# Sixteen of 22 gate-and-up column pairs of a SwiGLU feed-forward as seven block products instead of eight, in a float32 encoder trunk on one core

## The chip, the cores and the metric

The kernel runs on one core of one Trainium2 chip. Its time is the time on the device, in microseconds, from one launch; the median of three runs before the change is 2384.12 us (2383.22 to 2384.5). A profile of one execution goes with it.

## The reference

The program is an encoder trunk over one sequence of 512 tokens with 1024 features, all in float32. Two layers run one after the other. Each has a feed-forward, a mixer (a two-way state-space scan in the first layer, neighbourhood attention in the second), a second feed-forward, and a gated input from a side embedding:

```python
def rmsnorm(x, g):
    y = xf * lax.rsqrt(jnp.mean(xf * xf, axis=-1, keepdims=True) + RMS_EPS)
    return (y * g.astype(jnp.float32)).astype(x.dtype)

def swiglu(x, w_gu, w_down):
    g, u = jnp.split(x @ w_gu, 2, axis=-1)
    return (jax.nn.silu(g) * u) @ w_down

for i in range(DEPTH):                                        # DEPTH = 2
    h = h + 0.5 * swiglu(rmsnorm(h, ffn1_norm[i]), ffn1_w_gu[i], ffn1_w_down[i])
    hn = rmsnorm(h, mix_norm[i])
    h = h + (ssd_mixer(hn, ...) if i % 2 == 0 else neighbourhood_attention(hn, ...))
    h = h + 0.5 * swiglu(rmsnorm(h, ffn2_norm[i]), ffn2_w_gu[i], ffn2_w_down[i])
    gate = jax.nn.sigmoid(rmsnorm(h, ple_norm[i]) @ ple_w_gate[i])
    h = h + gate * rmsnorm(p[i] @ ple_w_proj[i], ple_post_norm[i])
```

The change concerns `swiglu`, which runs four times. `w_gu` is 1024 x 5632 (2816 gate columns, then 2816 up columns), `w_down` is 2816 x 1024.

## The kernel before

**Layout.** Features lie on the 128 partitions, tokens along the free axis. The residual stream is eight tiles `h[0..7]` of 128 x 512 (names `hs` in the profile). A weight "unit" is a 128 x 1024 tile: eight 128 x 128 blocks side by side.

**Three matmuls for one.** To keep float32 accuracy on a faster number format, each operand is held as a sum of two rounded parts, high and low. `split_unit` has ScalarE (ACT) cast a raw unit `wr` to its high part `wh` (line 166) and VectorE (DVE) subtract that from the raw unit to give the low part `wl` (line 168). Activations are split the same way into the two halves of an `md` tile (lines 189 and 190; with a gain, lines 192 and 193). For each 128 x 128 block `gemm` then issues three matmuls into one PSUM bank `ps`: high x high (line 181), weight high x activation low (line 184), weight low x activation high (line 185). TensorE (PE) takes its instructions strictly in order, so a low part that is late stops it at every third matmul.

**Weights.** `plan` lists all units in the order of use. `load_unit` issues the load of a unit on SyncE's DMA queue (SP) into one of four `wr` buffers. `unit()` hands out the next split unit and keeps up to three of them split ahead; `wh` and `wl` have three buffers each, so the split of a unit waits until the unit three before it is used up.

**A feed-forward.** The 2816 hidden columns are 22 tiles of 128, in chunks of 8, 7 and 7. For a tile f, `gate_up(f)` runs one gate unit and one up unit over the eight pairs of `norm.pairs` (the residual times the norm's gain, split), 24 matmuls of 128 x 512 each, into two banks. `activate` multiplies both by the factor `R` (one over the root mean square, in a tile `rt`; DVE, lines 313 and 317), applies SiLU on ACT (line 315), multiplies the two on GpSimd (POOL, line 318), and splits the result into `mids[f]`. `down(c)` multiplies the finished tiles of chunk c with `w_down`, one output tile d at a time, and adds half of it to `h[d]` (line 328). Chunk c's `down` runs after the gate and up units of chunk c+1. In the last `down`, `nxt(d)` prepares the next stage at once: it splits `h[d]` times the next gain and adds its square to a sum (ACT line 213, POOL line 217).

**The norm's factor.** `norm.factor()` sums over partitions with one plain float32 matmul (line 221) and runs a Newton iteration on 128 x 512 values. `norm.begin()` and `norm.end()` do the same on 128 x 4 values, with four small matmuls before (line 231) and four after it (line 241). Before, three of the feed-forwards use `factor`; the very first uses `begin` and `end`.

**Order.** The Tile framework puts the instructions of each engine into an order by their place in the code and by its own estimate of when they can run, assigns buffers from pools (24 `md`, 15 `sc`, 7 `t`, five PSUM banks of one tag and three of another), and makes the semaphores.

Of the kernel before, what the change touches and what calls it, by code (L numbers as in the profile page):

```python
# [21 lines left out]
CHUNKS = ((0, 8), (8, 15), (15, 22))  # L22
# [21 lines left out]
VAR = (0, 1, 1, 2)  # L44


@with_exitstack
def trunk(ctx, tc, A, out):
# [72 lines left out]
    def plan():  # L121
        for i in range(stop):
            l, w = divmod(i, 4)
            if w in (0, 2):
                gu, dn = (A["w_gu1"][l], A["w_dn1"][l]) if w == 0 else (A["w_gu2"][l], A["w_dn2"][l])
                for c, (a, b) in enumerate(CHUNKS):
                    for f in range(a, b):
                        yield gu[f, 0]
                        yield gu[f, 1]
                    for a, b in CHUNKS[max(c - 1, 0):c] + CHUNKS[-1:] * (c == len(CHUNKS) - 1):  # L130
                        if w == 2 and b == NF:
                            for n in range(2):
                                yield A["w_proj"][l, n]
                        for d in range(KD):
                            yield dn[d, :, a * P:b * P]
            elif w == 3:
                for n in range(KD):
                    yield A["w_gate"][l, n]
            elif l % 2 == 0:
                for n in range(65):  # L140
                    yield A["w_in"][n]
                for x in range(2):
                    for d in range(KD):
                        yield A["w_out"][d, :, x * 1024:(x + 1) * 1024]
            else:
                for n in range(24):
                    yield A["w_qkv"][n]
                for d in range(KD):
                    yield A["w_ao"][d]

    todo, raws, ready, splits = plan(), [], [], []

    def load_unit():
        src = next(todo, None)
# [6 lines left out]
    def split_unit():  # L161
        load_unit()
        if raws:
            raw, n = raws.pop(0)
            hi = wp.tile([P, 1024], F32R, name=nm("wh"), tag="wh", bufs=3)
            splits.append(s.copy(out=hi[:, :n], in_=raw[:, :n]))  # L166
            lo = wp.tile([P, 1024], F32R, name=nm("wl"), tag="wl", bufs=3)
            v.tensor_sub(out=lo[:, :n], in0=raw[:, :n], in1=hi[:, :n])  # L168
            ready.append((hi, lo))

    def unit():
        while len(ready) < 3 and (raws or not ready):
            split_unit()
        return ready.pop(0)

# [1002 lines left out]
```

## Time and profile before

| | |
|---|---|
| median of three runs | 2384.12 us |
| profiled execution, own time | 2384.19 us |
| its span, first to last instruction | 2382.4 us |
| matmuls on PE | 11464, PE busy 99% of the span |
| DVE, ACT, POOL busy | 59%, 40%, 19% |
| mean granted TensorE clock | 0.999 |
| DMA | 265.58 MB, mean 111 GB/s |

The profiled execution stands 0.07 us above the median of the runs; 1.8 us of its time lie outside the span. Matmuls are pipelined, so a matmul's own duration (392 ns for 128 x 512) is longer than the distance from one to the next, and PE's busy share says little; the distance between starts in the timeline is the better measure. "x3152" in a row is a count; the brackets in a timeline row give the idle time before it and what ended it.

### The profile page before, as it was taken

Reading aid. Unit: us, or ns where it says so; the run is one execution under the profiler, and the core shown is the slowest. Engines: PE = TensorE matmul, PEld = TensorE weight load, DVE = VectorE, ACT = ScalarE, POOL = GpSimd, SP = SyncE. Lnnn points to the kernel's source line nnn. Section 1 sums busy time; section 2 is a strip of 40 time slices with the busy share of each in tenths; the row PEclk is TensorE's granted clock in tenths of the full one; section 3 lists DMA queues with packets and bytes.
Section 4 is the critical chain, followed back from the end, with each engine's and each line's share of the span. In section 5 each row is a group of like instructions: output and inputs, shape, how many; then the busy total and the mean of one; then the engine's idle time right before and its main releaser. Section 6 shows DMA issues by size and latency. Waiting matters only on the chain.

```text
span 2382.4 us, 29262 instructions
## 1 busy us (share of the span) xinstructions
PE 2368.6 (99%) x11464; PEld 1953.0 (82%) x11464; DVE 1414.6 (59%) x1893; ACT 957.3 (40%) x1560; POOL 443.3 (19%) x373
## 2 busy tenths in 40 slices
PE   9999999999999999999999999999999999999999
PEld 8888888888888888888888788888877888888887
DVE  6453447877777858554446755444568855544456
ACT  5222324655555653322224433222337753322242
POOL 1110100444555541110103111000100011100120
PEclk9999999999999999999999999999999999999999
DMA  5333233544444452333333233333433332233332
GB/s 180 98 96 99 90 119 104 169 134 142 142 141 139 157 166 89 98 97 97 95 104 102 80 97 97 98 97 93 138 111 136 98 100 92 95 99 97 106 89 80
DMA packets 89707, 265.58 MB, mean 111 GB/s; under 512 B 10960, under 2 KB 11856, under 8 KB 89568
## 3 DMA queue, kind: packets, MB, share of 16 engines
q1 hardware_dynamic: 89280, 263.56, 35.0%
q8 instruction: 90, 1.47, 0.3%
q14 instruction: 49, 0.40, 0.1%
q10 hardware_dynamic: 288, 0.14, 0.0%
HBM read 253.40 MB, written 10.26 MB: 111 GB/s over the span
## 4 chain that ended last, share of the span: by engine, by line
PE 93%; DVE 4%; ACT 2%; issue 1%; DMA 1%; SPq 0%; POOL 0%; DVEq 0%; ACTq 0%; POOLq 0%
PE ps L181 28%; PE ps L184 28%; PE ps L185 28%; PE ps L657 1%; DVE wl L168 1%; PE ps L635 1%; PE ps L678 1%; PE ps L591 1%; PE ps L577 1%; PE ps L958 1%; PE ps L948 0%; DVE md L193 0%; DVE md L190 0%; PE ps L905 0%; PE ps L939 0%
## 5 line engine op out<-in xcount | busy, mean ns | idle before, releaser
L181 PE MATMUL ps<-md,wh 128*128 128x512 f32 (+1 forms) x3152 | 1236.7, 392 | 3.1 <-ACT md L192 3.1
L185 PE MATMUL ps<-md,wl 128*128 128x512 f32 (+1 forms) x3152 | 1228.5, 390 | 0.7 <-DVE wl L168 0.7
L184 PE MATMUL ps<-md,wh 128*128 128x512 f32 (+1 forms) x3152 | 1227.9, 390 | 0.3 <-DVE md L193 0.3
L166 ACT CAST wh<-wr 128x1024 fp32r<-128x1024 f32 (+1 forms) x401 | 414.7, 1034 | 1019.6 <-PE ps L184 638.7
L181 PEld LDWEIGHTS ps<-md,wh 128*128 128x128 f32 x3152 | 592.3, 188 | 128.2 <-issue 4.2
L184 PEld LDWEIGHTS ps<-md,wh 128*128 128x128 f32 x3152 | 592.3, 188 | 125.2 <-issue 4.9
L185 PEld LDWEIGHTS ps<-md,wl 128*128 128x128 f32 x3152 | 592.2, 188 | 124.9 <-DVE wl L168 1.3
L168 DVE TENSOR_TENSOR wl<-wr,wh 128x1024 fp32r<-128x1024 f32 (+1 forms) x401 | 576.8, 1438 | 157.5 <-ACT wh L166 131.8
L318 POOL TENSOR_TENSOR t<-t,sc 128x512 f32<-128x512 f32 x88 | 122.7, 1396 | 1033.0 <-ACT wh L166 635.4
L217 POOL TENSOR_TENSOR sq<-sq,sq 128x512 f32<-128x512 f32 x71 | 104.9, 1478 | 602.6 <-ACT sq L213 600.2
L317 DVE TENSOR_TENSOR t<-ps,rt 128x512 f32<-128x512 f32 x88 | 60.7, 690 | 258.6 <-PE ps L185 258.6
L328 DVE SCALAR_TENSOR_TENSOR hs<-ps,hs 128x512 f32<-128x512 f32 x96 | 66.3, 691 | 233.0 <-PE ps L185 233.0
L313 DVE TENSOR_TENSOR t<-ps,rt 128x512 f32<-128x512 f32 x88 | 60.8, 690 | 127.9 <-PE ps L185 125.6
L517 DVE SCALAR_TENSOR_TENSOR t<-ps,ccw,t 128x510 f32<-128x510 f32 (+1 forms) x180 | 134.0, 745 | 3.1 <-ACT t L513 0.3
L570 POOL TENSOR_TENSOR sc<-sc,sc 128x512 f32<-128x512 f32 x64 | 98.1, 1552 | 66.3 <-ACT sc L560 66.2
L189 ACT CAST md<-t 128x512 fp32r<-128x512 f32 x96 | 59.4, 623 | 121.3 <-POOL t L318 119.3
L558 ACT ACTIVATE sc<-hs,md 128x128 f32<-128x128 f32 x256 | 82.4, 396 | 2.9 <-DMA hs<-crow 2.9
L190 DVE TENSOR_TENSOR md<-t,md 128x512 fp32r<-128x512 f32 x96 | 67.9, 711 | 18.9 <-ACT md L189 18.4
L192 ACT ACTIVATE md<-hs,cst 128x512 fp32r<-128x512 f32 x64 | 46.0, 723 | 50.2 <-DVE hs L798 19.8
L520 ACT ACTIVATE t<-t 128x512 f32<-128x512 f32 x48 | 30.2, 630 | 78.6 <-DVE t L517 78.0
L585 POOL TENSOR_TENSOR md<-md,md 128x256 f32<-128x256 f32 x64 | 45.9, 751 | 84.1 <-ACT md L581 84.1
L193 DVE SCALAR_TENSOR_TENSOR md<-hs,cst,md 128x512 fp32r<-128x512 f32 x64 | 50.6, 794 | 13.7 <-ACT md L192 13.7
(169 smaller groups left out, 1366.7 us busy)
## 6 DMA issues: line engine op xcount, KB each, us to landing
wr<-in_w_gu_dram SPq DMA_DIRECT2D x172, 512.0 KB, 3.5
wr<-in_w_in_dram SPq DMA_DIRECT2D x65, 512.0 KB, 3.6
wr<-in_w_dn_dram SPq DMA_DIRECT2D x64, 448.0 KB, 3.3
wr<-in_w_dn_dram SPq DMA_DIRECT2D x32, 512.0 KB, 3.5
hs<-crow SPq DMA_DIRECT2D x64, 256.0 KB, 3.8
wr<-in_w_qkv_dram SPq DMA_DIRECT2D x24, 512.0 KB, 3.5
hs<-vrow SPq DMA_DIRECT2D x64, 128.0 KB, 4.0
wr<-in_w_out_dram SPq DMA_DIRECT2D x16, 512.0 KB, 4.2
```

The costliest lines, as they stand in the source:

```text
L166: splits.append(s.copy(out=hi[:, :n], in_=raw[:, :n]))
L168: v.tensor_sub(out=lo[:, :n], in0=raw[:, :n], in1=hi[:, :n])
L181: m = te.matmul(out=pt, lhsT=hi[:, sl], rhs=xp[:, 0, cols], start=first and k == 0, stop=False)
L184: te.matmul(out=pt, lhsT=hi[:, sl], rhs=xp[:, 1, cols], start=False, stop=False)
L185: te.matmul(out=pt, lhsT=lo[:, sl], rhs=xp[:, 0, cols], start=False, stop=last and k == n - 1)
L190: v.tensor_sub(out=dst[:, 1, :], in0=src, in1=dst[:, 0, :])
L217: (v if fast else g).tensor_add(out=self.acc, in0=self.acc, in1=q)
L318: g.tensor_mul(out=um, in0=um, in1=sg)
L328: v.scalar_tensor_tensor(out=h[d], in0=pt, scalar=0.5, in1=h[d], op0=ALU.mult, op1=ALU.add)
L517: v.scalar_tensor_tensor(out=a[:, lo:hi], in0=src[:, lo + o:hi + o], scalar=w(j), in1=a[:, lo:hi], op0=ALU.mult, op1=ALU.add)
L558: s.activation(out=e[:, cs(c)], in_=cb[:, cs(c)], func=AF.Relu, scale=-1.0, bias=cum[:, dr, c, hd:hd + 1])
L570: g.tensor_mul(out=es[j], in0=es[j], in1=cbm[j % 2])
```

## The change

In each feed-forward the chunks become 6, 6, 6 and 4 tiles. The six tiles of the first chunk ("plain") are computed as before. The other sixteen are taken as eight pairs p of neighbouring tiles. For a pair, the product of 1024 inputs x 512 columns (256 gate, 256 up) with 512 tokens is a 2 x 2 by 2 x 2 product of blocks, and it is computed with seven block products in place of eight (the scheme of Strassen and Winograd):

- The activation blocks and their sums are made once in a feed-forward, by `sums(kk)` for kk = 0 to 3, from `h[kk]` and `h[kk+4]` times gain and `R`: after plain tile 2 for kk = 0, after tile 3 for kk = 1, after tile 4 for kk = 2 and 3.
- The weight blocks are stored rearranged (`w_gw`): four 128 x 1024 units a pair, as before, from which DVE makes four sums (lines 216, 217, 218 and 223 of the new file, in `prep_next`). Seven units are then split in place of four.
- A block product (`block(p, i)`) is 24 matmuls of 128 x 256. DVE adds the seven results up from PSUM (line 461), ACT and POOL make SiLU and product, and `halve` splits the result into `mids` (lines 496 and 497).
- `ffn_order` sets the order: units of the second matrix of the chunk before stand between the block products, eight to a chunk; the last chunk's eight `down` products (now of 4 tiles, 12 matmuls each) come last.
- The first tile of a feed-forward, and the first two tiles of the attention, run their two units side by side: `side_by_side` does the first seven pairs for both banks and the eighth pair for both at the end. Feed-forwards now all use `begin` and `end` for the factor.
- In `activate`, SiLU is done in place.

Line numbers move: 181, 184, 185 are 246, 249, 250 after; 166, 168 are 195, 197; 313, 317 are 393, 396; 328 is 515; the block products are lines 455 to 457.

```diff
-CHUNKS = ((0, 8), (8, 15), (15, 22))
+CHUNKS = ((0, 6), (6, 12), (12, 18), (18, 22))
+PLAIN = CHUNKS[0][1]
+HT = T // 2
+def ffn_order():
+    for f in range(PLAIN):
+        yield "plain", f
+    for c in range(1, len(CHUNKS)):
+        a, b = CHUNKS[c]
+        blocks = [(p, i) for p in range(a // 2, b // 2) for i in range(7)]
+        d = 0
+        for n, (p, i) in enumerate(blocks):
+            yield "block", p, i
+            while d < KD and (d + 0.5) * len(blocks) <= KD * (n + 1):
+                yield "down", c - 1, d
+                d += 1
+    yield "between",
+    for d in range(KD):
+        yield "down", len(CHUNKS) - 1, d
...
-    def split_unit():
-        load_unit()
-        if raws:
-            raw, n = raws.pop(0)
...
+    def prep_next():
+        item = next(todo, None)
...
+        if what == "u":
+            load_unit()
+            split_raw(*raws.pop(0))
+        elif what == "g":
+            while len(raws) < 4:
+                load_unit()
+            a21, a22, a11, a12 = [raws.pop(0)[0] for _ in range(4)]
+            s1, s2, s3 = wide(), wide(), wide()
+            v.tensor_add(out=s1, in0=a21, in1=a22)
+            v.tensor_sub(out=s2, in0=s1, in1=a11)
+            v.tensor_sub(out=s3, in0=a11, in1=a21)
+            blocks.update({0: a11, 1: s2, 2: s3, 3: s1, 4: a12, 6: a22})
+        else:
+            if a == 3:
+                blocks[5] = wide()
+                v.tensor_sub(out=blocks[5], in0=blocks[4], in1=s_of[0])
...
+            split_raw(blocks.pop(a), 1024)
+            if len(raws) < 3:
+                load_unit()
...
     def unit():
-        while len(ready) < 3 and (raws or not ready):
-            split_unit()
+        while len(ready) < 3 and prep_next():
+            pass
         return ready.pop(0)
...
+    def side_by_side(pts, pairs, behind=False):
+        ws = [unit() for _ in pts]
+        k = len(pairs) - 1
+        for pt, w in zip(pts, ws):
+            gemm(pt, w, pairs[:k], last=False, behind=behind)
+            behind = False
+        for pt, w in zip(pts, ws):
+            gemm(pt, w, pairs[k:], first=False, off=k)
...
+            if f == 0 and not first:
+                side_by_side((pg, pu), norm.pairs)
+                norm.begin()
...
-            if R[0] is None:
-                R[0] = norm.factor()
...
+        def sums(kk):
+            lo_, hi_ = slice(0, HT), slice(HT, T)
+            x = []
+            for k in (kk, kk + 4):
+                x.append(t2())
+                v.scalar_tensor_tensor(out=x[-1], in0=h[k], scalar=col(norm.gain + k), in1=R[0], op0=ALU.mult,
+                                       op1=ALU.mult)
...
+            s.copy(out=hl[0], in_=x[0][:, lo_])
+            v.tensor_sub(out=hl[1], in0=x[0][:, lo_], in1=hl[0])
+            xs[0][kk] = hl
+            pr = md(F32R)
+            split(pr, x[1], None)
...
+            a, b = t2(), t2()
+            v.tensor_sub(out=a[:, lo_], in0=x[0][:, hi_], in1=x[0][:, lo_])
+            v.tensor_sub(out=b[:, lo_], in0=x[1][:, hi_], in1=x[0][:, hi_])
+            v.tensor_sub(out=a[:, hi_], in0=x[1][:, hi_], in1=a[:, lo_])
+            v.tensor_sub(out=b[:, hi_], in0=x[1][:, lo_], in1=a[:, hi_])
+            for x_, hh, ll in ((a, ah, al), (b, bh, bl)):
+                s.copy(out=hh, in_=x_)
+                v.tensor_sub(out=ll, in0=x_, in1=hh)
...
+        def block(p, i):
+            pt = mm_bank()
+            hi, lo = unit()
+            for j in range(2):
+                for kk in range(4):
+                    sl = slice((4 * j + kk) * P, (4 * j + kk + 1) * P)
+                    o = pt[:, j * HT:(j + 1) * HT]
+                    xh, xl = xs[i][kk]
+                    te.matmul(out=o, lhsT=hi[:, sl], rhs=xh, start=j == 0 and kk == 0, stop=False)
+                    te.matmul(out=o, lhsT=hi[:, sl], rhs=xl, start=False, stop=False)
+                    te.matmul(out=o, lhsT=lo[:, sl], rhs=xh, start=False, stop=j == 1 and kk == 3)
```

**The order on DVE where the plain tiles end.** The place is the third feed-forward of the program (the first of layer 1). In the names, `t` and `sc` are scratch, `wr` a raw unit, `wl` the low part of a split unit, `md` a pair or a weight sum, `hs` the residual, `rt` the factor. Before, DVE's work on a plain tile is five rows that repeat (here eight rows of two neighbouring tiles):

```order
L317 TENSOR_TENSOR t_11294<-ps_11229,rt_10773 128x512
L168 TENSOR_TENSOR wl_11306<-wr_11188,wh_11304 128x1024
L190 TENSOR_TENSOR md_11297<-t_11294,md_11297 128x512
L313 TENSOR_TENSOR t_11362<-ps_11300,rt_10773 128x512
L168 TENSOR_TENSOR wl_11336<-wr_11230,wh_11334 128x1024
L317 TENSOR_TENSOR t_11366<-ps_11301,rt_10773 128x512
L168 TENSOR_TENSOR wl_11378<-wr_11260,wh_11376 128x1024
L190 TENSOR_TENSOR md_11369<-t_11366,md_11369 128x512
```

After, from the split of the first block product's unit (`wl_13055`) past that of the second (`wl_13085`) to that of the first `down` unit (`wl_13127`):

```order
L197 TENSOR_TENSOR wl_13055<-wr_12959,wh_13053 128x1024
L437 TENSOR_TENSOR t_13034<-t_13024,t_13033 128x256
L440 TENSOR_TENSOR md_13031<-t_13033,md_13031 128x512
L216 TENSOR_TENSOR md_13047<-wr_12865,wr_12929 128x1024
L440 TENSOR_TENSOR md_13032<-t_13034,md_13032 128x512
L217 TENSOR_TENSOR md_13048<-md_13047,wr_12959 128x1024
L218 TENSOR_TENSOR md_13049<-wr_12959,wr_12865 128x1024
L393 TENSOR_TENSOR t_13113<-ps_13043,rt_12688 128x512
L197 TENSOR_TENSOR wl_13085<-md_13048,wh_13083 128x1024
L396 TENSOR_TENSOR t_13116<-ps_13044,rt_12688 128x512
L223 TENSOR_TENSOR md_13189<-wr_13045,md_13048 128x1024
L265 TENSOR_TENSOR md_13119<-t_13116,md_13119 128x512
```

Between the two splits now stand the last of the activation sums (437, 440), three weight sums (216 to 218) and the scaling of plain tile 5 (393). Ahead of the first of them, back to plain tile 4's scaling of its up product (396), stand nineteen more rows of `sums(2)`, `sums(3)` and `activate`: six of 128 x 512 and nine of 128 x 256 with two operand tiles, and four scaling ones of 128 x 512.

**The order on PE there.** `ps_13122` is the bank of the first block product, `ps_13155` of the second, `ps_13188` of the first `down`. Before, only products of 128 x 512 stand here. After, the start of each:

```order
L455 MATMUL ps_13122<-md_12813,wh_13053 128x256
L456 MATMUL ps_13122<-md_12813,wh_13053 128x256
L457 MATMUL ps_13122<-md_12813,wl_13055 128x256
L455 MATMUL ps_13122<-md_12813,wh_13053 128x256
```

and, at the end of the second block product,

```order
L457 MATMUL ps_13155<-md_13031,wl_13085 128x256
L246 MATMUL ps_13188<-md_12726,wh_13125 128x512
L249 MATMUL ps_13188<-md_12726,wh_13125 128x512
L455 MATMUL ps_13214<-sc_12821,wh_13156 128x256
L456 MATMUL ps_13214<-sc_12822,wh_13156 128x256
L455 MATMUL ps_13247<-sc_12819,wh_13191 128x256
L456 MATMUL ps_13247<-sc_12820,wh_13191 128x256
L250 MATMUL ps_13188<-md_12726,wl_13127 128x512
```

Each product's third matmul needs the low part `wl`; the first `down` has two matmuls ahead of it, and two each of the next two block products are put between.

**The order on PE at the start of that feed-forward.** `ps_10708` and `ps_10707` are up and gate of tile 0 before, `ps_12569` and `ps_12570` the two after. The pair `md_10701` before, `md_12563` after, is the eighth, made last by the stage ahead. Before:

```order
L181 MATMUL ps_10707<-md_10701,wh_10619 128x512
L181 MATMUL ps_10708<-md_10427,wh_10662 128x512
L184 MATMUL ps_10707<-md_10701,wh_10619 128x512
L185 MATMUL ps_10707<-md_10701,wl_10621 128x512
L184 MATMUL ps_10708<-md_10427,wh_10662 128x512
L185 MATMUL ps_10708<-md_10427,wl_10664 128x512
```

After:

```order
L246 MATMUL ps_12570<-md_12515,wh_12524 128x512
L249 MATMUL ps_12570<-md_12515,wh_12524 128x512
L250 MATMUL ps_12570<-md_12515,wl_12526 128x512
L246 MATMUL ps_12569<-md_12563,wh_12481 128x512
L249 MATMUL ps_12569<-md_12563,wh_12481 128x512
L250 MATMUL ps_12569<-md_12563,wl_12483 128x512
L246 MATMUL ps_12570<-md_12563,wh_12524 128x512
L249 MATMUL ps_12570<-md_12563,wh_12524 128x512
L250 MATMUL ps_12570<-md_12563,wl_12526 128x512
L306 MATMUL ps_12631<-ones_d,sq_12292 128x1 x4
```

The eighth pair was used 21 matmuls into the stage; now it is used after 42. The plain matmul over 512 tokens (221) has gone, and four matmuls of 128 x 1 (306) stand in its place, with four of 128 x 128 (line 316) one unit later.

195 lines of the change are left out of this document (141 added, 54 removed).

## The prediction

> **What bounds the kernel now.** I read the page's busy times and its chain first, then one feed-forward by stretches, then PE's timeline.
>
> ```profile
> span 2382.4 us, 29262 instructions
> PE 2368.6 (99%) x11464; PEld 1953.0 (82%) x11464; DVE 1414.6 (59%) x1893; ACT 957.3 (40%) x1560; POOL 443.3 (19%) x373
> PE 93%; DVE 4%; ACT 2%; issue 1%; DMA 1%; SPq 0%; POOL 0%; DVEq 0%; ACTq 0%; POOLq 0%
> ...
> 939.00:1141.00 202.00, 202.00 (x893) 167.22 (x892) 102.98 (x103) 57.52 (x69) 19.38 (x15) 1.00 0.32 97
> ```
>
> PE holds 93% of the chain, and in the gate-and-up stretch of the second feed-forward it never idles while DVE is half free. So a feed-forward lasts as long as its matmuls take from start to start:
>
> ```profile
> 2349.73 0.39 PE L184 MATMUL ps<-md,wh 128*128 128x512 f32 x1
> ...
> 2371.94 0.28 PE L181 MATMUL ps<-md,wh 128*128 128x256 f32 x1
> ...
> 2377.57 0.28 PE L185 MATMUL ps<-md,wl 128*128 128x256 f32 x1
> ...
> L181 PE MATMUL ps<-md,wh 128*128 128x256 f32 x16 | 4.5, 283 | 0.0
> ```
>
> From 2349.73 to 2371.94 are 98 matmuls of 128 x 512: 226.7 ns each. The last weight unit is used in two halves, 48 matmuls of 128 x 256 (three lines of 16); 47 steps take 5.63 us, 120 ns each. That is more than half of 226.7: a narrow matmul wastes about 13 ns more in every two.
>
> **Block products.** A pair of tiles is 96 matmuls x 226.7 = 21.76 us before, and 7 x 24 = 168 matmuls x 120 = 20.16 us after: 1.60 us saved, not the 2.72 us that an eighth would be. 8 pairs x 4 feed-forwards: **-51.2 us**. The `down` matmuls keep their number.
>
> The Trainium skill ("TensorE: Matmul & The Clock Gate", section Back-to-back issue gap) puts the warm distance at N/2.4 + 2.5 ns, 215.8 and 109.2 here; by that, an estimate, the saving would be 2.37 us a pair, 76 us in all. Both rows lie 11 ns above it, so I go by the rows.
>
> **DVE in the steady blocks.** DVE's prices, start to start, come from rows where it runs without a pause:
>
> ```profile
> 380.77 2.72 DVE L452 SCALAR_TENSOR_TENSOR t<-hs,cst,rt 128x512 f32<-128x512 f32 x4
> 383.42 2.48 DVE L190 TENSOR_TENSOR md<-t,md 128x512 fp32r<-128x512 f32 x4
> ...
> 393.28 1.21 DVE L168 TENSOR_TENSOR wl<-wr,wh 128x1024 fp32r<-128x1024 f32 x1
> 394.42 0.74 DVE L517 SCALAR_TENSOR_TENSOR t<-t,ccw,t 128x511 f32<-128x511 f32 x1
> 395.08 0.41 DVE L465 SCALAR_TENSOR_TENSOR sc<-sc 128x256 f32<-128x256 f32 x1
> 395.41 0.74 DVE L517 SCALAR_TENSOR_TENSOR t<-t,ccw,t 128x511 f32<-128x511 f32 x1
> ...
> 967.26 1.22 DVE L168 TENSOR_TENSOR wl<-wr,wh 128x1024 fp32r<-128x1024 f32 x1 [0.21 <-ACT wh L166]
> 972.70 2.30 DVE L168 TENSOR_TENSOR wl<-wr,wh 128x1024 fp32r<-128x1024 f32 x1 [0.21 <-ACT wh L166]
> ...
> 972.63 1.29 POOL L318 TENSOR_TENSOR t<-t,sc 128x512 f32<-128x512 f32 x1 [9.59 <-DVE t L317]
> ...
> L168 DVE TENSOR_TENSOR wl<-wr,wh 128x1024 fp32r<-128x1024 f32 x24 | 42.5, 1772 | 5.1 <-ACT wh L166 5.1
> ```
>
> So 1.14 us for 1024 columns (394.42 less 393.28), 0.60 for 512, 0.66 scaled, 0.33 for 256; 0.87 for 768, halfway between 512 and 1024. POOL's product beside a split makes it 1.08 us longer. A pair needs 7 splits and 4 weight sums (11 x 1.14), 7 additions and 2 halves (9 x 0.60), two POOL products (2 x 1.08), and with 8/3 `down` units (0.87 + 0.60 each) 24.0 us; were every wide row at the mean of 1.77 us, 28.8. PE needs 20.16 + 8/3 x 18 x 0.2267 = 31.0. PE stays the bound, by 2 to 7 us a pair. The weight sums come in a burst, though: where no `down` stands between the first products of a new pair, the second one's split (after 4 wide rows, two halves, two POOL products) comes about 0.5 us late, once in each feed-forward: **+2** (0 if POOL misses it, 8 if the loads add a wait).
>
> **The first blocks are late.** Tile 5's 48 matmuls give DVE 10.88 us to make the sums of kk = 2 and 3. From tile 4's last matmul to the first product's split are 6 x 0.60 + 4 x 0.66 + 9 x 0.33 + 1.14 + 1.08 (POOL) = 11.4 us; PE wants it at its third matmul, 11.1: 0.3 late. The second split follows after 0.33 + 3 x 0.60 + 4 x 1.14 = 6.7, at 18.1; PE wants it at 14.3: 3.8 late. The first `down`'s split follows after 2 x 0.60 + 1.14 + 0.87 + 1.08 = 4.3, at 22.4; PE, pushed back, wants it at 21.7: 0.7 late. Sum 4.8 us. In the first feed-forward `R` comes only during tile 2,
>
> ```profile
> 40.11 0.69 DVE L313 TENSOR_TENSOR t<-ps,rt 128x512 f32<-128x512 f32 x1 [2.14 <-ACT rt L244]
> ```
>
> so three tiles' scaling (six rows of 0.60, three halves, three POOL products of 1.29) crowds into tile 3's 10.88 us together with the sums of kk = 0; I put what is left over at 1.4, between 0 and 4. 3 x 4.8 + 6.2 = **+20.7 us**. Below: 0, if DVE starts on the sums with time in hand. Above: 10 us each, if the six wide rows in it take the mean of 1.77 us (+3.8) and seven of them wait 0.21 us for ACT's cast, as the brackets show now (+1.5). I take the rows that run freely, since POOL has one product here and not the many that make that mean.
>
> Who waits behind these: PE's whole queue stands behind each third matmul, and on DVE the additions that free the PSUM banks stand behind the sums. Five banks hold five products, so that costs nothing more before PE is five products (14 us) ahead.
>
> **Loads.** A pair still has four loads of 512 KB, and SP's queue keeps its order; what moves is when a buffer comes free.
>
> ```profile
> wr<-in_w_gu_dram SPq DMA_DIRECT2D x172, 512.0 KB, 3.5
> ```
>
> Of the four `wr` buffers one is held from a pair's first sum to its fifth product's split and one to its seventh's, so meanwhile all loads share two, and in SP's queue a load that waits holds up those behind it. A load that is issued when a split ends lands 3.5 us later; the units split ahead last PE 2 x 2.88 = 5.8 us. I cost it at nothing, hidden by those two units; were they used up, each pair would pay up to 3.5 us, which belongs to the third rival. SiLU in place and the attention's two tiles side by side (its first tiles show no wait for the eighth pair now) cost nothing either; ACT's seven casts a pair at 1.05 us are 7.4 of 31 us.
>
> **Starts.**
>
> ```profile
> 1348.84 0.39 PE L185 MATMUL ps<-md,wl 128*128 128x512 f32 x1
> 1352.32 0.73 PE L181 MATMUL ps<-md,wh 128*128 128x512 f32 x2 [3.09 <-ACT md L192]
> ...
> 1357.09 0.39 PE L181 MATMUL ps<-md,wh 128*128 128x512 f32 x1
> ...
> 1352.00:1357.00 5.00, 4.63 (x12) 3.38 (x13) 2.58 (x3) 1.84 (x3) 0.00 (x0) 0.66 0.22 85
> ...
> 373.89 0.95 PE L231 MATMUL ps<-ones_d,sq 128*128 128x1 f32 x8
> 374.70 0.49 PE L181 MATMUL ps<-md,wh 128*128 128x512 f32 x1
> ...
> 378.38 1.13 PE L241 MATMUL ps<-msk,sm 128*128 128x128 f32 x8
> 379.26 0.48 PE L181 MATMUL ps<-md,wh 128*128 128x512 f32 x1
> ...
> 938.05 1.02 PE L221 MATMUL ps<-sq,ones_d 128*128 128x512 f32 x2
> 938.50 0.80 PE L181 MATMUL ps<-md,wh 128*128 128x512 f32 x1
> 939.14 0.40 PE L184 MATMUL ps<-md,wh 128*128 128x512 f32 x1
> ```
>
> At the third feed-forward PE waits 3.25 us (3.48 less one step) for the eighth pair, and the granted clock then falls to 0.66: 12 matmuls take 4.77 us for 2.72, 2.05 more. Side by side, 21 more matmuls (4.76 us) go ahead of that pair: **-5.3 us**. `begin` and `end` cost PE 0.81 + 0.88 = 1.69 us; `factor` costs 0.45, and 0.41 in the step behind it: 0.83 more, three times, **+2.5**.
>
> **Ends.** In the last chunk PE has 2.72 us for an output tile where it had 4.76, and each tile still needs:
>
> ```profile
> 346.66 0.74 DVE L193 SCALAR_TENSOR_TENSOR md<-hs,cst,md 128x512 fp32r<-128x512 f32 x1
> ...
> 346.96 1.58 POOL L217 TENSOR_TENSOR sq<-sq,sq 128x512 f32<-128x512 f32 x1 [3.18 <-ACT sq L213]
> 349.61 0.69 DVE L328 SCALAR_TENSOR_TENSOR hs<-ps,hs 128x512 f32<-128x512 f32 x1 [2.21 <-PE ps L185]
> ```
>
> DVE's 0.60 + 0.60 + 0.66 alone fits; with POOL's 1.58 wholly against it, it is 3.44 and falls 5.7 us behind in eight tiles. The next stage wants the eighth pair after 21 matmuls (4.76) where it isn't side by side (three of four ends). I take 1 us at each, **+3**, between 0 and 10.
>
> Sum: -51.2 + 20.7 + 2 - 5.3 + 2.5 + 3 = -28.3. The profiled execution took 2384.19 us (1.8 of it outside the span), 0.07 above the median of the runs: 2355.9, so **2356 us**.
>
> **Rivals.**
> - *DVE keeps up* at the first blocks: without the 20.7, 2335. For it: DVE is half idle before; against it, the sum of rows above. 0.14.
> - *The late blocks are dearer*: 10 us each (+21 - in all 2376), and PE's clock falls there as at 1352, 2.05 us each (+8): 2364 to 2384. The Trainium skill (same page, Part 1: The HAM clock gate) has the clock halve after an idle window of about 3.4 us; the trace's one such wait, 3.25 us, agrees. Against it: the 3.8 us are broken by two matmuls. 0.17.
> - *Slower*: DVE, in order, stands in the steady blocks behind the halves, which wait for an addition, SiLU, POOL and a cast in turn, and every pair loses. 28.3/32 = 0.9 us a pair is where the gain is gone; at 1.5 us it is 2404. For it:
>
> ```profile
> DVE wl L168 <- ACT wh L166: 131.8, 234, 5.6
> ```
>
> DVE already stands 131.8 us in 234 waits for casts. Against it: PE has two units split ahead, 5.8 us, and DVE 2 to 7 us a pair to spare. 0.12.
> - *Narrow matmuls lose their fixed part* in a long stream: half of 226.7 is 113.3 ns, 6.7 less than 120; 168 x 32 x 6.7 ns are 36 us, which gives 2320. The 48 rows at 120 ns, all of one stream, speak against it. 0.03. (By the skill's distances above, as an estimate, it would be 2331.)
> - *The gain is no gain*: smaller stalls of several kinds leave within 0.2% (4.8 us, about what a measurement of this kernel tells from nothing). 0.06.
>
> **Numbers.** The forecast has 0.48, with 2346 to 2367 as its own range. The range reaches to DVE keeping up, 2334, and to the dear late blocks, 2384, which leaves out some 0.18. Faster: the forecast, DVE keeping up, the faster matmul and most of the dear case, 0.80; same 0.08; slower 0.12.
>
> **What will show it.** Starts of the block products' matmuls (455 to 457) 120 ns apart; a wait of 3 to 5 us at line 457 for the low part (line 197) once in each feed-forward, in the first pair; no wait at 457 in later pairs above 1 us; the 3.09 us wait at the third feed-forward gone. Wrong, if PE waits for DVE in each pair, or if the narrow matmuls don't keep 120 ns.

## The result: slower by 2.9%, and the profile after

The changed kernel takes 2452.7 us (median of four runs, 2451.2 to 2454.53), the kernel before 2384.31: a ratio of 1.0288, 95% interval 1.027 to 1.0306. The forecast was 2356, with a range up to 2384. It was wrong by 97 us, and on the wrong side.

The head of the page of the changed kernel, its chain, and two of its groups (busy time and mean, then the idle time ahead of them and what ended it):

```profile
span 2449.2 us, 34985 instructions
PE 2367.2 (97%) x13810; PEld 2049.9 (84%) x13810; DVE 1771.3 (72%) x2437; ACT 1105.3 (45%) x1787; POOL 476.3 (19%) x373
...
PE 76%; DVE 12%; ACT 4%; POOL 4%; issue 2%; DMA 1%; SPq 0%; ACTq 0%; POOLq 0%; DVEq 0%
...
L455 PE MATMUL ps<-sc,wh 128*128 128x256 f32 x768 | 222.6, 290 | 14.3 <-ACT wh L195 14.3
L457 PE MATMUL ps<-sc,wl 128*128 128x256 f32 x768 | 221.2, 288 | 12.6 <-DVE wl L197 12.6
```

PE's share of the chain fell from 93% to 76%; DVE, ACT and POOL now hold a fifth of it. PE waits for casts (`wh`) and low parts (`wl`), and it does so at fixed places. (Other groups and rows are left out at the three dots, here and below.) The table adds up, from PE's timeline, by how much the distance from one matmul's start to the next exceeds 226.7 ns (128 x 512) or 120 ns (128 x 256). This is called PE's loss here, and a slow clock counts in it. The last column takes in all from a feed-forward's last block product to the first two units of the next stage, the side embedding's units among them.

| PE's loss, us | pair 1 | 2 | 3 | 4 | 5 | 6 | 7 | 8 | last `down` |
|---|---|---|---|---|---|---|---|---|---|
| first feed-forward | 8.4 | 1.9 | 0.1 | 1.8 | 1.9 | 0.1 | 5.7 | 6.9 | 0.0 |
| second | 6.9 | 1.9 | 0.1 | 1.8 | 1.9 | 0.1 | 6.2 | 7.4 | 8.3 |
| third | 7.5 | 1.9 | 0.1 | 1.8 | 1.9 | 0.1 | 6.2 | 7.3 | 0.0 |
| fourth | 7.0 | 2.5 | 0.1 | 1.8 | 1.9 | 0.1 | 6.0 | 7.2 | 8.2 |

First pairs: 29.8 us. The seven others, four times: 76.3. Ends: 16.5. With the 51.2 us that the block products save and the 3.7 by which the span is shorter with the rest of the change alone (`starts`, below), -51.2 - 3.7 + 29.8 + 76.3 + 16.5 is +67.7; the spans differ by 66.8. So the account is complete to 0.9 us, and its largest entry is one that the prediction had at 2. Part of the loss is a slow clock: up to the last matmuls the granted clock stood at one half for 75 us of this span in all, and for 3.4 us before. At half the clock that costs at most half the time, an estimate from these numbers: 37 of the 122.6 us of loss.

**An ordinary boundary between pairs.** PE, DVE, ACT and POOL in the timeline, where the second pair of the second feed-forward begins (start, duration, instruction, and in brackets the idle time before it and what ended it):

```profile
1049.20 0.39 PE L455 MATMUL ps<-sc,wh 128*128 128x256 f32 x1 [0.62 <-ACT wh L195]
...
1050.45 0.39 PE L457 MATMUL ps<-sc,wl 128*128 128x256 f32 x1 [0.76 <-DVE wl L197]
...
1042.83 0.69 DVE L497 TENSOR_TENSOR md<-t,md 128x512 fp32r<-128x512 f32 x1 [1.84 <-ACT md L496]
1043.44 1.22 DVE L216 TENSOR_TENSOR md<-wr,wr 128x1024 f32<-128x1024 f32 x1
1044.58 0.68 DVE L461 TENSOR_TENSOR t<-ps,t 128x512 f32<-128x512 f32 x1
1045.18 1.21 DVE L217 TENSOR_TENSOR md<-md,wr 128x1024 f32<-128x1024 f32 x1
1046.31 2.31 DVE L218 TENSOR_TENSOR md<-wr,wr 128x1024 f32<-128x1024 f32 x1
...
1047.58 0.62 ACT L496 CAST md<-t 128x512 fp32r<-128x512 f32 x1 [4.78 <-POOL t L491]
1048.10 1.99 ACT L195 CAST wh<-md 128x1024 fp32r<-128x1024 f32 x2
...
1045.34 2.21 POOL L491 TENSOR_TENSOR t<-t,t 128x512 f32<-128x512 f32 x1 [3.19 <-DVE t L461]
```

Read it from DVE: it stands 1.84 us before the first half's subtraction (L497), which waits for ACT's cast, which waits for POOL's product. The three weight sums of the next pair (L216 to L218) stand behind that, though the sums need nothing from it. The addition for the second half (L461) stands among the sums, so POOL's second product starts late, and while it runs L218 takes 2.31 us for 1.22. ACT meanwhile waits 4.78 us for that product, and the casts of the next two units (1048.10) stand behind it.

At pairs 3 and 6 next to nothing is lost (0.06 us, 0.1 in the table). At the third pair of the same feed-forward, whose first matmul starts at 1075.79, DVE stands the same 1.84 us before the first half (L497), but the sums were made before:

```profile
1065.59 1.22 DVE L217 TENSOR_TENSOR md<-md,wr 128x1024 f32<-128x1024 f32 x1
...
1068.46 1.22 DVE L218 TENSOR_TENSOR md<-wr,wr 128x1024 f32<-128x1024 f32 x1
...
1078.33 0.69 DVE L497 TENSOR_TENSOR md<-t,md 128x512 fp32r<-128x512 f32 x1 [1.84 <-ACT md L496]
```

The third sum ends 6.1 us before the pair's first matmul; at pair 2, whose first matmul starts at 1045.55, it ends 3.1 us after it (1048.62). In this feed-forward the third sum ends 6.1 us ahead at pairs 3 and 6, and 2.0 to 3.1 us late at the other five. So the framework's order on DVE differs from pair to pair, and the loss goes with it.

**A costly boundary.** The same at the last pair of that feed-forward, where the second unit is one of the second matrix:

```profile
1255.09 0.79 PE L246 MATMUL ps<-md,wh 128*128 128x512 f32 x1 [4.32 <-ACT wh L195]
...
1254.20 0.83 ACT L195 CAST wh<-wr 128x768 fp32r<-128x768 f32 x1 [2.81 <-DMA wr<-in_w_dn_dram]
...
1248.50 2.31 DVE L218 TENSOR_TENSOR md<-wr,wr 128x1024 f32<-128x1024 f32 x1
...
1250.84 5.54 SPq L190 DMA_DIRECT2D wr<-in_w_dn_dram  x3
```

All four raw buffers hold the next pair. The load of the `down` unit is issued at 1250.84, just when L218, the last reader of one of them, ends (1250.81); ACT waits for it, and PE 4.32 us for ACT.

### The profile page after: what moved, and what is told of

Its sections match the earlier page's. It is cut to its first block, busy times and chain, and to the rows that moved or that the text cites. A ratio compares the mean times of both kernels' runs of the same rounds, so it can differ in the third digit from the quotient of the medians.

```text
span 2449.2 us, 34985 instructions
## 1 busy us (share of the span) xinstructions
PE 2367.2 (97%) x13810; PEld 2049.9 (84%) x13810; DVE 1771.3 (72%) x2437; ACT 1105.3 (45%) x1787; POOL 476.3 (19%) x373
## 4 chain that ended last, share of the span: by engine, by line
PE 76%; DVE 12%; ACT 4%; POOL 4%; issue 2%; DMA 1%; SPq 0%; ACTq 0%; POOLq 0%; DVEq 0%
PE ps L250 17%; PE ps L246 17%; PE ps L249 16%; PE ps L455 7%; PE ps L457 7%; PE ps L456 7%; POOL t L491 2%; DVE wl L197 2%; ACT wh L195 2%; DVE md L218 2%; DVE md L216 1%; PE ps L833 1%; DVE md L217 1%; PE ps L811 1%; PE ps L854 1%
## 5 line engine op out<-in xcount | busy, mean ns | idle before, releaser
L246 PE MATMUL ps<-md,wh 128*128 128x512 f32 x2128 | 848.5, 399 | 36.2 <-ACT wh L195 31.9
L250 PE MATMUL ps<-md,wl 128*128 128x512 f32 x2128 | 838.9, 394 | 5.8 <-DVE wl L197 5.8
L249 PE MATMUL ps<-md,wh 128*128 128x512 f32 x2128 | 838.9, 394 | 0.2
L195 ACT CAST wh<-wr 128x1024 fp32r<-128x1024 f32 (+2 forms) x401 | 385.4, 963 | 648.1 <-PE ps L249 313.1
L197 DVE TENSOR_TENSOR wl<-wr,wh 128x1024 fp32r<-128x1024 f32 (+2 forms) x401 | 466.7, 1164 | 153.5 <-ACT wh L195 127.2
L457 PE MATMUL ps<-md,wl 128*128 128x256 f32 x1024 | 291.7, 285 | 4.4 <-DVE wl L197 4.4
L456 PE MATMUL ps<-md,wh 128*128 128x256 f32 x1024 | 291.1, 284 | 0.0
L455 PE MATMUL ps<-md,wh 128*128 128x256 f32 x1024 | 290.8, 284 | 0.0
L455 PE MATMUL ps<-sc,wh 128*128 128x256 f32 x768 | 222.6, 290 | 14.3 <-ACT wh L195 14.3
L457 PE MATMUL ps<-sc,wl 128*128 128x256 f32 x768 | 221.2, 288 | 12.6 <-DVE wl L197 12.6
L461 DVE TENSOR_TENSOR t<-ps,t 128x512 f32<-128x512 f32 x224 | 151.4, 688 | 108.3 <-PE ps L457 107.4
L456 PE MATMUL ps<-sc,wh 128*128 128x256 f32 x768 | 219.3, 286 | 0.0
L195 ACT CAST wh<-md 128x1024 fp32r<-128x1024 f32 x128 | 131.7, 1047 | 109.1 <-PE ps L456 68.6
```

Of the source, the lines that this page charges most:

```text
L246: m = te.matmul(out=pt, lhsT=hi[:, sl], rhs=part(xp, 0, cols), start=first and k == 0, stop=False)
L249: te.matmul(out=pt, lhsT=hi[:, sl], rhs=part(xp, 1, cols), start=False, stop=False)
L250: te.matmul(out=pt, lhsT=lo[:, sl], rhs=part(xp, 0, cols), start=False, stop=last and k == n - 1)
L455: te.matmul(out=o, lhsT=hi[:, sl], rhs=xh, start=j == 0 and kk == 0, stop=False)
L456: te.matmul(out=o, lhsT=hi[:, sl], rhs=xl, start=False, stop=False)
L457: te.matmul(out=o, lhsT=lo[:, sl], rhs=xh, start=False, stop=j == 1 and kk == 3)
```

## The experiments

Names: `starts`, `late` and so on are kernels. "The changed kernel" is 2452.7 us; before was 2383.3 to 2383.9 in these comparisons.

**`starts`: the rest of the change alone.** Diff from the changed kernel: all tiles plain, chunks of before.

```diff
-CHUNKS = ((0, 6), (6, 12), (12, 18), (18, 22))
+CHUNKS = ((0, 8), (8, 15), (15, 22))
...
```

> This kernel leaves the block products out: all 22 tiles are plain, in the chunks of before (8, 7, 7); only the rest of the change is in it (two units side by side at the starts, the 128 x 4 factor, SiLU in place). The prediction's terms for this part are -5.3 us (third feed-forward's start) and +2.5 us (the factor's matmuls): about 2381.5. If the starts or the factor are where the changed kernel loses, it takes over 2390; if they do nothing, 2384.

Measured: 2380.45 us, ratio 0.9989 (0.998 to 0.9998); that is 2.8 us less than before in the same comparison, and the profiled span is 3.7 us shorter. From the second feed-forward's last output tile to the third's are 406.3 us, for 410.7 before: there the gain is. The loss is all with the block products and the chunks that go with them.

**`late`: ACT's queue.** The cast and subtraction of a pair's second half come after the first product of the next pair, and the cast is kept in that place.

```diff
-                halve(k["hl"], x, c)
+                if i == 5 or p == NF // 2 - 1:
+                    halve(k["hl"], x, c)
+                else:
+                    later.append((k["hl"], x, c, True))
+            if i == 0:
+                while later:
+                    halve(*later.pop(0))
```

> The changed kernel with ScalarE's cast of a pair's last half moved behind the casts of the next pair's units (it waits for GpSimd's product, and they stood behind it). Theory Q (ScalarE's queue): in the changed kernel PE loses 1.9 us at four pair boundaries of each feed-forward and 6 to 7 us at two, and that cast is what holds the queue at all six: the four go, the two shrink by 2 us each, 4 x (7.5 + 4) = 46 us less, about 2407. Theory L (loads: a unit of the second matrix can't be loaded before the weight sums free one of the four raw buffers): the two large ones stay, at most 4 x 4 = 16 us less, 2437. Theory D (DVE has too much work in all): no change, 2450 to 2455.

Measured: 2441.61 us, 11 less than the changed kernel; 46 were expected of theory Q. The cast did move, yet pairs 2 and 5 lose 1.9 us as before. DVE and ACT of this kernel at the same boundary:

```profile
1040.76 0.69 DVE L506 TENSOR_TENSOR md<-t,md 128x512 fp32r<-128x512 f32 x1 [1.84 <-ACT md L503]
1041.37 1.22 DVE L216 TENSOR_TENSOR md<-wr,wr 128x1024 f32<-128x1024 f32 x1
...
1043.10 1.22 DVE L217 TENSOR_TENSOR md<-md,wr 128x1024 f32<-128x1024 f32 x1
1044.23 2.32 DVE L218 TENSOR_TENSOR md<-wr,wr 128x1024 f32<-128x1024 f32 x1
...
1047.08 2.34 DVE L197 TENSOR_TENSOR wl<-md,wh 128x1024 fp32r<-128x1024 f32 x2
...
1044.43 1.05 ACT L195 CAST wh<-md 128x1024 fp32r<-128x1024 f32 x1 [3.70 <-DVE md L217]
...
1048.34 0.39 PE L458 MATMUL ps<-sc,wl 128*128 128x256 f32 x1 [1.59 <-DVE wl L197]
```

ACT is free now, but the cast waits for the sum L217, and the sums still stand behind the *first* half. The cast ends at 1045.48; its unit's split on DVE starts only at 1047.08, behind the third sum, and PE waits 1.59 us for that (PE's row is the last of the fence; its line 458 is 457 of the changed kernel). Theory Q had the wrong queue.

**`wr5`: five raw buffers.** `tag="wr", bufs=4` becomes `bufs=5`, and an unused filler tile shrinks to make room.

> The changed kernel with five raw-weight buffers in place of four. Theory L: the two large waits of each feed-forward (6 and 7 us with the slow clock behind them) go nearly whole, 4 x 11 = 44 us less, about 2409. Theory Q: the load was not what the cast waited for, at most 8 us less, 2445. Theory D: 2450 to 2455.

Measured: 2402.52 us, 50 less. Pairs 7 and 8 now lose 1.8 and 1.5 us, pairs 2 and 5 still 1.9. That is theory L's place, and nearly its number: pairs 7 and 8 give back 40 us of the 44; the first pairs give 7.0 and pair 4 gives 3.7.

**`dveprod`: the product on DVE.** `g.tensor_mul(out=x, in0=x, in1=gate)` becomes `v.tensor_mul(...)`.

> The changed kernel with the product of gate and up of a pair (64 of 128 x 512) made by DVE in place of GpSimd: 0.6 us each on DVE in place of 1.7 to 2.2 us on GpSimd, which made a DVE row beside it 1.1 us longer. Theory Q: the chain from the addition to the cast is 1.5 us shorter at six boundaries of each feed-forward, 24 x 1.5 = 36 us less, about 2417. Theory L: the sums end 1.1 us sooner where the product ran beside them, 8 x 1.1 = 9 us less, about 2444. Theory D: DVE has 64 x (1.1 - 0.6) = 32 us less to do, 2440 to 2450.

Measured: 2408.68 us, 44 less, though DVE has more instructions of its own. Pairs 2 and 5 lose 0.1 to 0.2 us; pairs 7 and 8 still 3.3 to 5.3. Of the three times forecast, theory Q's 2417 is the nearest: the chain from the addition to the cast does count, though it holds DVE's queue and not ACT's. At pair 2 of the second feed-forward the third sum now ends 1.5 us after the pair's first matmul, for 3.1.

**`downs`: other places for the second matrix's units.**

```diff
-            while d < KD and (d + 0.5) * len(blocks) <= KD * (n + 1):
+            if n + 1 in DOWNS[len(blocks)]:
...
+DOWNS = {21: (3, 5, 8, 10, 12, 15, 17, 19), 14: (1, 2, 3, 5, 8, 9, 10, 12)}
```

> The changed kernel (four buffers, product on GpSimd) with the units of the second matrix at other places between the block products: after the 3rd and 5th of a chunk's first pair, the 1st, 3rd and 5th of the others, and the 1st, 2nd, 3rd and 5th in the last chunk, so that none stands on a pair's boundary or just ahead of it. In the changed kernel PE loses 0.06 us at the one boundary of this form (third pair of a chunk). Theory L: the others become like it, 4 x 12 = 48 us less, about 2405. Theory D: no change, 2445 to 2455.

Measured: 2394.31 us, 58 less, with the same buffers and the same work. Pairs 2 to 6 lose 0.04 to 0.06 us, pair 7 1.3 to 1.4, pair 8 0.1, so the loss isn't set by how much DVE has to do: theory D falls. It doesn't tell loads from order, though: in the second feed-forward the third sum now ends 5.8 to 6.1 us before the first matmul at every pair. New losses take back some 15 us. The largest, 5.6 us in the second and fourth feed-forward, stands right behind the last product: the side embedding's first matmul waits 5.44 us for a cast (line 265 there) which stands on ACT behind the last half.

**`late2`: both halves behind the sums.** As `late`, but for the first half too:

```diff
-                if i == 5 or p == NF // 2 - 1:
+                if p == NF // 2 - 1:
```

> The changed kernel (four buffers, product on GpSimd) with the casts of both halves of a pair behind the casts of the next pair's first units, so that DVE's subtractions, which wait for them, no longer stand ahead of the next pair's weight sums. When the second half's cast alone was moved, 10 us went and PE still lost 1.9 us at the ordinary boundaries: there DVE stood 1.8 us idle before the first half's subtraction, with the sums behind it. If that order on DVE is the cause, the 1.2 to 1.9 us boundaries fall under 0.3 and the two large ones by 2 us each: 4 x 9 = 36 us less than the changed kernel, about 2416. If GpSimd's product, which makes a DVE row beside it 1.1 us longer, is the cause, it still does: at most 12 us less, 2440.

Measured: 2376.12 us, ratio to before 0.9966 (0.9952 to 0.998): 77 us less than the changed kernel, where 36 were expected, with four buffers and the product still on POOL. Pairs 2 to 8 lose 0.03 to 0.30 us. DVE at this boundary, then ACT and POOL:

```profile
1022.99 1.23 DVE L217 TENSOR_TENSOR md<-md,wr 128x1024 f32<-128x1024 f32 x1 [1.02 <-DMA wr<-in_w_gw_dram]
...
1024.73 1.22 DVE L218 TENSOR_TENSOR md<-wr,wr 128x1024 f32<-128x1024 f32 x1
1025.86 2.33 DVE L197 TENSOR_TENSOR wl<-wr,wh 128x1024 fp32r<-128x1024 f32 x1
...
1034.76 1.29 DVE L506 TENSOR_TENSOR md<-t,md 128x512 fp32r<-128x512 f32 x2
...
1034.11 1.14 ACT L503 CAST md<-t 128x512 fp32r<-128x512 f32 x2
...
1028.87 2.22 POOL L492 TENSOR_TENSOR t<-t,t 128x512 f32<-128x512 f32 x1 [1.76 <-DVE t L462]
```

The sums end at 1025.95, and both halves follow at 1034 without a wait. POOL's product still takes 2.22 us and still stretches a row to 2.33: that costs nothing here. The order on DVE and ACT alone was worth 74 of the 76.3 us, the loads included, and 3 more at the ends. The edit moved the two halves, and the framework then also set the sums earlier: in the second feed-forward the third sum ends 4.0 to 6.1 us before the first matmul at every pair. At its last pair that is 1215.90 for a first matmul at 1220.80, and the load of the `down` unit is issued at 1215.92; in the changed kernel both came 3.1 us after that matmul. Where the sums come in time, the buffers come free in time. `downs` has sums as early as these; `wr5` and `dveprod` leave the sums of pairs 2, 4, 5, 7 and 8 late and make other links of the chain shorter. Why the framework sets the sums early at some pairs and late at others is not shown.

**`both`, and the first blocks.** `both` has five buffers and the product on DVE; `firstb` also makes the activation sums one plain tile earlier in the last three feed-forwards:

```diff
-                    for kk in ((0,), (1,), (2, 3), ())[a[0] - 2]:
+                for kk in (((), (), (0,), (1,), (2, 3), ()) if first else ((), (0,), (1,), (2,), (3,), ()))[a[0]]:
```

> The changed kernel with five raw buffers and the pairs' product on DVE. Theory LP (two causes, loads and GpSimd's product, at different boundaries): with five buffers 8 us a feed-forward are left at the later pairs, nearly all at boundaries which the product on DVE clears (0.1 and 0.5 there), so 4 x 6.5 = 26 us less than with five buffers alone (2402.5): about 2376, and at the pairs after the first one PE loses under 2 us in a feed-forward. Theory D (what is left is DVE's whole amount of work): the two don't add up, 2392 to 2402.

Measured: 2371.56 us, ratio 0.9948 (0.9934 to 0.9963). Pairs 2 to 8 lose 1.0 to 1.3 us together in a feed-forward, and the time is 31 us below that of `wr5`, where 26 were expected: the two add up. (Alone they gave 50 and 44, together 81: both shorten pairs 7 and 8.)

> The kernel with five buffers and the product on DVE, and the activations' sums one plain tile earlier in the last three feed-forwards (one in each of tiles 1 to 4 in place of tiles 2, 3 and two in 4). The prediction's step on the first blocks (DVE has 11.4 us of rows in 10.9 us, then 6.7 and 4.3): with half of them gone the first pair's loss (4.4 to 7.0 us) falls under 1 us in these three, 3 x 5 = 15 us less than without it. If the loss comes from something else (GpSimd's product of the plain tiles, buffers, loads), less than 5 us.

Measured: 2353.44 us, ratio 0.9872 (0.9858 to 0.9887), 18 less than `both`. The first pair loses 0.07 us in each of the three (5.1 to 5.9 in `both`), and still 7.0 in the first feed-forward, whose sums were not moved. In the changed kernel (first fence; PE, then DVE) the split of the first product's unit comes 0.75 us late; for the second PE waits 2.08 us for the cast and 1.21 for the split; in `firstb` (second fence; PE, then DVE) the first split ends at 986.16, 3.9 us before PE's third matmul, and the rows of PE stand 120 ns apart:

```profile
1007.35 0.39 PE L457 MATMUL ps<-md,wl 128*128 128x256 f32 x1 [0.75 <-DVE wl L197]
...
1012.32 0.39 PE L455 MATMUL ps<-sc,wh 128*128 128x256 f32 x1 [2.08 <-ACT wh L195]
...
1014.03 0.38 PE L457 MATMUL ps<-sc,wl 128*128 128x256 f32 x1 [1.21 <-DVE wl L197]
...
1006.08 1.22 DVE L197 TENSOR_TENSOR wl<-wr,wh 128x1024 fp32r<-128x1024 f32 x1
...
1012.76 1.21 DVE L197 TENSOR_TENSOR wl<-md,wh 128x1024 fp32r<-128x1024 f32 x1
```

```profile
990.10 0.28 PE L457 MATMUL ps<-md,wl 128*128 128x256 f32 x1
990.22 0.28 PE L455 MATMUL ps<-md,wh 128*128 128x256 f32 x1
...
984.94 1.22 DVE L197 TENSOR_TENSOR wl<-wr,wh 128x1024 fp32r<-128x1024 f32 x1
...
991.62 1.22 DVE L197 TENSOR_TENSOR wl<-md,wh 128x1024 fp32r<-128x1024 f32 x1
```

**`ends` and `ends2`: the last output tiles.** Both start from a kernel above. `ends` makes the chunks 6, 6, 4, 6; `ends2` works out the side embedding's factor on 128 x 4 values:

```diff
-CHUNKS = ((0, 6), (6, 12), (12, 18), (18, 22))
+CHUNKS = ((0, 6), (6, 12), (12, 16), (16, 22))
```

```diff
-            r3 = ss.rsqrt(4.0, 4.0 * EPS)
+            ss.begin(4.0, 4.0 * EPS)
+            r3 = ss.end()
```

> The kernel with five buffers and the product on DVE, and the chunks 6, 6, 4, 6 in place of 6, 6, 6, 4: the last output tiles have 4.08 us of matmuls each in place of 2.72. If the second and fourth feed-forward lose at their ends (8.2 us each in the changed kernel) because an output tile is too short for DVE's rows beside it, 2 x 5 = 10 us less than the kernel of the same call without it; if the loss is the two units of the side embedding that wait for the last pair, 2 x 2 = 4 us less; if neither, the same.

Measured: 2373.45 us, no better than `both` (2371.56). The loss at the second and fourth end did go, from 5.8 to 2.4 and 2.7 us, but it came back just ahead: 3.8 us at pair 8 and 1.0 more at pair 7. PE and ACT there:

```profile
1248.03 0.70 PE L246 MATMUL ps<-md,wh 128*128 128x512 f32 x1 [3.61 <-ACT md L264]
...
1246.84 0.62 ACT L496 CAST md<-t 128x512 fp32r<-128x512 f32 x1 [1.63 <-DVE t L491]
1247.36 1.14 ACT L264 CAST md<-md 128x512 fp32r<-128x512 f32 x2
```

The side embedding's cast (L264) stands on ACT behind the last half, which waits: the same pattern on another queue.

> The kernel with five buffers, the product on DVE and the earlier sums (2353.4), and the factor of the side embedding's norm, which DVE works out on 128 x 512 values beside the last output tiles of the second and fourth feed-forward, on 128 x 4 values. If those wide rows (some eleven of 0.6 us, two or three of them 1.1 us longer beside GpSimd's sums) are what makes DVE late at these ends (5.1 and 5.8 us lost), 2 x 3.5 = 7 us less: 2346. If DVE's own rows of an output tile are too much for 2.72 us, or the wait for the last pair is what counts, at most 2 us less.

Measured: 2348.6 us, 4.8 less than `firstb`; the two ends lose 3.3 us each, for 5.1 and 5.8. The intervals overlap (0.9838 to 0.9871 against 0.9858 to 0.9887), so it is the loss in the trace, more than the time, that says the wide rows were part of it. In the changed kernel, DVE's rows there, 1.1 us longer beside POOL, and the wait that they cause on PE:

```profile
1321.63 0.68 DVE L280 SCALAR_TENSOR_TENSOR rt<-sc,rt 128x512 f32<-128x512 f32 x1
1322.23 1.78 DVE L268 SCALAR_TENSOR_TENSOR md<-hs,cst,md 128x512 fp32r<-128x512 f32 x1
...
1331.72 0.50 PE L250 MATMUL ps<-md,wl 128*128 128x512 f32 x1 [2.06 <-DVE wl L197]
```

**`adp` and `best`.** `adp` is `firstb` with the plain tiles' product on DVE as well; `best` is `adp` with the change of `ends2`.

> The kernel with five buffers, the product on DVE and the earlier sums (2353.4), and the product of gate and up of the plain tiles on DVE too. Only the first feed-forward still loses at its first pair (7.0 us): three tiles' scaling waits there for the factor. Each product on GpSimd makes a DVE row 1.1 us longer and on DVE takes 0.6: six of them, 3 us less, and the chain to the sums is a little shorter: 2349 to 2351. If GpSimd's product isn't in the way there, no change, or 1 to 3 us more for DVE's added rows.

Measured: 2351.73 us, 1.7 less than `firstb`, and the intervals overlap (0.9851 to 0.988 against 0.9858 to 0.9887). The first pair of the first feed-forward loses 4.5 us for 7.0, but `ends2`, in which nothing was changed there, shows 5.8. The waits tell more than the sums: PE's wait for the first product's split is 2.21 and 2.19 us in `firstb` and `ends2`, and 0.90 and 0.91 in `adp` and `best`. So the product on DVE does take 1.3 us off this wait; the rest of the scatter goes with the clock, which fell once at this place in the other three and not in `adp`. The gain in time is not settled.

> Both of these changes together with the five buffers, the product on DVE and the earlier sums: 2353.4 - 7 - 3 = 2343 if both do what the first readings say; 2350 to 2354 if neither does. What is then left over the block products' own saving (2384 - 51 - 4 = 2329) is the first feed-forward's first pair, about 4 us, and the rest of the ends.

Measured: 2347.55 us, ratio to before 0.9848 (0.9834 to 0.9863): 36 us faster than before and 105 faster than the changed kernel, between the two forecasts. What is left over the block products' own saving is 5.4 us at the first feed-forward's first pair, 1.0 us at the other pairs of each, and 3.3 at two ends.

## Why the prediction was wrong, point by point

- **Block products, -51.2: right.** In `late2` and `best` the loss in pairs 2 to 8 is 0.03 to 0.33 us a pair, against 120 ns for each of 168 matmuls, so the narrow matmuls keep their distance, and the fourth rival (a shorter fixed part) falls.
- **DVE in the steady blocks, +2: this step failed.** It measured 76.3, the loads included. The step set 24.0 us of DVE's rows a pair against PE's 31.0 and saw room. The sum of work was no bound (`downs` and `late2` do the same work), the order was. The prediction allowed half a microsecond for the burst of weight sums, once in each feed-forward. It counted the two halves in that burst as rows of work, and left out their waits: each waits for a chain over three engines (1.84 us at pair 2), and the sums stood behind.
- **Loads at nothing: failed too, as a follower.** The prediction said that a pair's sums hold the raw buffers, and relied on two units split ahead. At two boundaries of each feed-forward that cover was used up, and the load was the last link (2.81 us on ACT for the DMA).
- **The slower rival named the mechanism.** "DVE, in order, stands in the steady blocks behind the halves" is what the chip shows, with 76.3/32 = 2.4 us a pair for the 1.5 in the text, and 2452.7 for 2404. It isn't every pair, as the rival had it: pairs 3 and 6 lose 0.1, and 53 of the 76.3 us stand at pairs 7 and 8, where the load adds its wait. It got a chance of 0.12 because of the two averages: two units ahead, and 2 to 7 us to spare a pair. Neither says what happens at the boundary, where the sums, the halves and the `down` unit meet.
- **First blocks, +20.7: mechanism right, size 29.8.** The row count gave 0.3 us at the first product, 3.8 at the second and 0.7 at the first `down`; in the second feed-forward the starts slip by 0.91 at the first product and by 2.24 and 1.37 at the second, and the first `down` isn't late. That is 4.5 for 4.8, with some luck in the parts. What was left out of the sum is the rest, 2.4 us of the 6.9: the slow clock behind it (the second rival had 2.05) and a wait of 0.3 us at the third product. The first feed-forward lost 8.4 for 6.2. `firstb` shows the cause, and the rival that DVE keeps up falls.
- **Starts, -5.3 and +2.5: right in sum**, `starts` is 2.8 us faster. From the second feed-forward's end to the third's it gains 4.4 us, for 5.3 less 0.8. Of the 0.8 us that the second and the fourth were to lose, 0.0 and 0.7 show, so the second term is borne out in part.
- **Ends, +3: measured 16.5.** The term counted three or four DVE rows for an output tile. It left out the embedding's factor, whose wide rows run beside the last tiles, and the embedding's cast behind the last half.
- **What was to show it:** 120 ns held, the 3.09 us wait is gone, the wait at the first pair is there, in three parts. "No wait at 457 in later pairs above 1 us" held too, by its letter: the longest is 0.76 us. The sign looked at one line. The waits are for casts as well (0.62 us at 455 beside the 0.76), and the long ones stand at 246, on the unit behind (4.32 us at 1255). What came is nearly the sign of being wrong: PE waits in five of the seven later pairs.

## What to carry to other kernels

On an engine that works in order, compare not sums of work but what stands ahead of the rows that the bound engine needs next: a row that waits for a chain over other engines must not stand ahead of work that is ready. A burst at the boundary of a loop is priced at the boundary, with the cover that is left there, and not as its mean over the loop. When one order is wrong, several remedies (more buffers, a faster link, other places) each seem to be the cause; the one that leaves all resources as they were, as `late2` did, tells. And where a loop loses at some turns and not at others, compare the order at a good turn with that at a bad one first: here pairs 2 and 3 of the changed kernel already showed it.

## What the runs showed of the hardware

**The clock fell after waits of 2 us, where they fell into one stretch of 3.41 us.** The prediction knew one wait of 3.25 us. In the changed kernel, stretches of the second feed-forward (length, busy times and counts of PE, PEld, DVE, ACT, POOL, then the granted clock):

```profile
1011.84:1015.25 3.41, 1.72 (x12) 1.52 (x13) 3.41 (x5) 1.53 (x3) 0.53 (x1) 1.00 0.52 164
1015.25:1018.66 3.41, 3.41 (x16) 3.17 (x16) 1.58 (x3) 2.60 (x4) 1.60 (x1) 0.50 0.17 67
...
1206.40:1209.81 3.41, 1.75 (x15) 1.54 (x13) 2.42 (x3) 0.00 (x0) 2.04 (x1) 1.00 0.47 131
1209.81:1213.22 3.41, 1.15 (x4) 0.71 (x5) 2.07 (x3) 3.25 (x5) 0.13 (x1) 1.00 0.25 100
1213.22:1216.64 3.42, 3.42 (x9) 2.67 (x9) 1.93 (x2) 0.48 (x1) 0.00 (x0) 0.50 0.41 115
...
1291.73:1295.14 3.41, 1.51 (x7) 1.18 (x7) 1.94 (x4) 2.18 (x4) 0.78 (x1) 1.00 0.28 77
1295.14:1298.56 3.42, 3.42 (x10) 2.67 (x9) 1.15 (x2) 0.85 (x2) 0.00 (x0) 0.50 0.30 79
```

After waits of 2.08 and 1.21 us, and after one of 1.90 (to 1293.74), the clock is at 0.50 for 3.41 us, and it starts 1.2 and 1.4 us after PE is busy again, so the slow matmuls stand well behind the wait that caused them. The delay isn't a constant. In this trace all 18 falls of the clock lie a whole multiple of 3.413 us apart, to 0.01 us (from 1015.25 to 1213.22 are 58 of them, to 1295.14 another 24), and so do the falls in every other run that has more than one. Cut along this grid, the changed kernel's stretches at full clock divide by PE's busy time: after 1.72 us or less of 3.41 the next one is slow, after 1.75 or more it isn't. Over all runs the border is less sharp: with PE busy for less than 0.45 of a stretch the clock always fell, with more than 0.58 never. So by these traces it counts how much of a wait falls into one stretch of the grid, and the same wait can be free in one execution and cost a slow stretch in another, as at the first pair in `adp` and `best`.

The Trainium skill ("TensorE: Matmul & The Clock Gate", Part 1: The HAM clock gate) states an idle window of about 3.4 us as what brings the half clock; the slow stretch of 3.41 us agrees with that length, but here waits shorter than that were enough.
